# Three split fp32r passes for the second expert product, and an earlier start of the gathered rows

## The chip, the cores and the metric

The kernel runs on one core of one Trainium2 chip. The metric is the device time of one execution in microseconds. The kernel before was timed in three runs: 2528.99, 2518.30 and 2519.91 us, median 2519.91.

## The reference

256 tokens with 2048 features pass through two layers. The first layer and the first part of the second are projections, a gated convolution, causal attention over 8 heads, a 31-tap convolution and a state-space recurrence. The change does not touch them, save for one loop named below. It concerns the last part, a product-key mixture of single-neuron experts:

```python
def peer(h, w_q, sub_keys, u_tab, v_tab):     # h (B,S,2048); both tables 16384 x 2048
        q = (xb @ w_q).reshape(PEER_TOKEN_BLOCK, PEER_HEADS, 2, PEER_HALF)
        s = jnp.einsum('thcd,hcnd->thcn', q, sub_keys).astype(jnp.float32)
        s_top, i_top = lax.top_k(s, PEER_TOPK)
        ...
        best, pos = lax.top_k(cand, PEER_TOPK)
        expert = jnp.take_along_axis(cand_idx, pos, axis=-1)
        gates = jax.nn.softmax(best, axis=-1).astype(xb.dtype)
        u_sel = u_tab[expert]
        v_sel = v_tab[expert]
        act = jax.nn.gelu(jnp.einsum('td,thkd->thk', xb, u_sel))
        return jnp.einsum('thk,thkd->td', gates * act, v_sel)
```

Each token takes 16 experts in each of 8 heads. The result is added to the residual and normalised once more (gain `gfin`).

## The kernel before

**Two ways through the experts.** The first 88 tokens (`NS_`) are done sparsely: for every token and chosen expert the row of the u table and later the row of the v table is gathered from HBM. One gather (`gather`, L1416, an indirect DMA on GpSimd's queue) brings 128 rows, a [128, 2048] buffer of 1 MB. For a u row VectorE forms a dot product with the token's row (L1449); for a v row it adds the row, times its weight, to a sum `acc_s` (L1461, L1463). `GROUPS` puts 32, 32, 16 and 8 tokens on 128 partitions, so there are 88 u gathers and 88 v gathers, in batches of four, a v batch one batch behind its u batch. The other 168 tokens (`NT`) are done densely: all 16384 experts in 128 tiles of 128. `u_step` (L1577) multiplies u tile i with the tokens, 16 matmuls into one bank, and ScalarE applies the gelu (L1580). `weigh` (L1391, L1395) multiplies by a gate table, zero where a token did not choose an expert. `v_step` (L1594) multiplies v tile i with these weights, 16 matmuls into 16 sums `acc[d]`, which stay open in six PSUM banks for all 128 tiles.

**Number formats.** Earlier weight tiles are split: ScalarE copies the tile to an fp32r part (`w_hi`, L189), VectorE subtracts it and writes the fp32r rest (`w_lo`, L195), and a product is hi x hi + hi x lo + lo x hi. `mm_perm` (L278 to L280) does that with three matmuls of 256 columns; `mm_wide` (L293, L294) with one of 512 columns, both activation parts side by side, and one of 256. The expert tiles are not split: they are listed in `whole`, and their products are single f32 matmuls of 168 columns, each of which the chip executes as two instructions.

**Order.** Everything is written out in order by a generator scheduler. `step` first issues loads and splits that lie ahead (`w_ahead`; `LDH` and `LDL` say how far), then the step's matmuls, then lets background generators run: `weave.run`, and `run_paced`, which gives the sparse generator `sparse` 0.78 of a 2350 ns row product per step. Each engine takes its instructions in that order. Weight tiles arrive by SyncE's queue (`w_load`, L183) in the order of the list `order`: 58 u tiles (`NU0`), then v and u tiles in turn until the u tiles end, then v tiles alone. Five raw buffers (`NR`) go round; a buffer is loaded again once the matmuls of its tile have run.

**What precedes the expert stage.** 16 query projection tiles (two in `first_tiles`, 14 by `mm_wide`), then per head the key scores and the top-16 search on VectorE (`topk`, `picks`), first for tokens 0 to 127 (`tt` = 0). After the last head `hand_out` sends expert numbers and later gate values to the gather lists, and `sp_start` begins gathering into five buffers. `gbuild` builds the gate table of the dense tokens by matmuls (L1375), 128 of the 168 tokens through HBM (`gd`), from where `gload` brings back 16 expert tiles at a time.

**The end.** The sparse sums of the last two groups are added to `y` by `join_rows` through PSUM banks 0 and 1; it needs these banks, which the u product also uses, so it asserts that the u product has ended (`u_done`). The last two v tiles are multiplied bank by bank, with transposes and sums of squares between (L1666, L1673), then the rows are scaled and stored.

## Time and profile before

| | |
|---|---|
| runs | 2528.99, 2518.30, 2519.91 us; median 2519.91 |
| profiled execution | 2530.83 us, span from first to last instruction 2528.9 us |
| mean granted TensorE clock | 0.991 |
| HBM read, written | 687.10 MB, 25.91 MB |
| DMA | 719.91 MB, mean 285 GB/s |
| u products (L1577) | 4096 instructions, first at 1229.0 us, last at 2220.0 |
| v products (L1594) | 4096 instructions, first at 1545.4 us, last at 2512.6 |

The profile shows one execution. Its engines are PE (matmuls) and PEld (weight loads) of TensorE, DVE (VectorE), ACT (ScalarE), POOL (GpSimd) and SP (SyncE, DMA issue only). A group's line gives busy time and the mean of one instruction, then the idle time just before its instructions with what ended it. Matmuls overlap in the pipeline, so the time that one takes from its neighbours is the distance of starts, not its duration. In a timeline consecutive instructions of one line are merged (x32), and the first start and the total are shown.

### The profile page before, as it was taken

To read this page: it belongs to the slowest core of one execution; us is meant where nothing else is said; L and a number is where in the kernel's file an instruction comes from. 1 tells how busy PE (TensorE), PEld (TensorE's weight loads), DVE (VectorE), ACT (ScalarE), POOL (GpSimd) and SP (SyncE) were. 2 spreads that over 40 slices of the span, in tenths; PEclk is the share of its full clock that TensorE was granted. 3 is DMA by queue.
4 is the path that set the end of the run, shared out by engine and by line. 5 is a ranking of instruction groups with operands and counts; after the bars stand their busy time and mean duration, and the time that the engine had idled before them with its cause. 6 is when DMAs were issued, how large, how long until landed. Compare 5 with 4: busy or idle time off the path is not lost.

```text
span 2528.9 us, 40512 instructions
## 1 busy us (share of the span) xinstructions
PE 2445.0 (97%) x16864; PEld 2322.2 (92%) x16864; DVE 1586.5 (63%) x2764; ACT 700.2 (28%) x1047; POOL 657.0 (26%) x856
## 2 busy tenths in 40 slices
PE   8999999999999999999998999999999999999997
PEld 7888878899999999988998999999999999999887
DVE  6857777589999987657768874534453434324423
ACT  5544455443334445454201640000000000000002
POOL 1788888310000000140122121212122312022000
PEclk9999999999999999999999999999999999999998
DMA  6455555565555444555599999999999999999983
GB/s 237 168 199 184 183 183 210 193 238 210 199 206 179 183 168 181 185 202 193 215 336 418 370 380 417 421 382 421 418 421 415 396 386 414 365 344 398 387 259 125
DMA packets 108187, 719.91 MB, mean 285 GB/s; under 512 B 13308, under 2 KB 14572, under 8 KB 24668
## 3 DMA queue, kind: packets, MB, share of 16 engines
q1 hardware_dynamic: 65764, 474.57, 49.9%
q0 software_dynamic: 34288, 220.73, 22.3%
q10 hardware_dynamic: 7952, 22.02, 2.4%
q8 instruction: 133, 2.18, 0.3%
q14 instruction: 50, 0.41, 0.0%
HBM read 687.10 MB, written 25.91 MB: 282 GB/s over the span
## 4 chain that ended last, share of the span: by engine, by line
PE 71%; DMA 19%; DVE 7%; issue 2%; ACT 1%; POOL 1%; SPq 0%; DVEq 0%; POOLq 0%; ACTq 0%
PE b L1577 14%; PE b L293 13%; PE b L1594 12%; DMA s<-in_vexp_dram 7%; PE b L294 7%; DMA s<-in_wst_dram 6%; PE b L278 4%; PE b L280 4%; PE b L279 4%; DVE s L195 2%; PE b L271 2%; PE b L423 2%; PE b L270 2%; PE b L269 2%; DMA s<-s 2%
## 5 line engine op out<-in xcount | busy, mean ns | idle before, releaser
L1577 PE MATMUL b<-s,s 128*128 128x168 f32 x4096 | 609.2, 308 | 14.0 <-DMA s<-in_wst_dram 13.6
L1594 PE MATMUL b<-s,s 128*128 128x168 f32 x4096 | 605.1, 307 | 17.3 <-DMA s<-in_vexp_dram 15.9
L1594 PEld LDWEIGHTS b<-s,s 128*128 128x128 f32 x4096 | 588.3, 190 | 30.4 <-issue 27.0
L1577 PEld LDWEIGHTS b<-s,s 128*128 128x128 f32 x4096 | 590.6, 191 | 21.4 <-issue 20.4
L293 PE MATMUL b<-s,s 128*128 128x512 f32 x1680 | 599.7, 400 | 0.0
L294 PE MATMUL b<-s,s 128*128 128x256 f32 x1680 | 472.0, 281 | 9.6 <-DVE s L195 9.6
L195 DVE TENSOR_TENSOR s<-s,s 128x2048 fp32r<-128x2048 f32 x192 | 453.3, 2363 | 27.2 <-issue 12.5
L293 PEld LDWEIGHTS b<-s,s 128*128 128x128 f32 x1680 | 316.1, 188 | 72.8
L189 ACT ACTIVATE s<-s 128x2048 fp32r<-128x2048 f32 x192 | 365.7, 1905 | 9.6 <-DMA s<-in_wst_dram 9.1
L1449 DVE CUSTOM_DVE_ANT_0 s<-s,s 128x2048 f32<-128x2048 f32 x88 | 201.1, 2290 | 261.0 <-DMA s<-in_uexp_dram,rbuf 209.9
L294 PEld LDWEIGHTS b<-s,s 128*128 128x128 f32 x1680 | 317.7, 189 | 13.8 <-DVE s L195 13.0
L1463 DVE SCALAR_TENSOR_TENSOR s<-s,sqsum,s 128x2048 f32<-128x2048 f32 x84 | 197.4, 2350 | 120.8 <-DMA s<-in_vexp_dram,rbuf 120.3
L1580 ACT ACTIVATE s<-b 128x168 f32<-128x168 f32 x128 | 39.1, 307 | 803.7 <-PE b L1577 803.7
L278 PE MATMUL b<-s,s 128*128 128x256 f32 x896 | 256.6, 286 | 0.0
L280 PE MATMUL b<-s,s 128*128 128x256 f32 x896 | 253.5, 283 | 0.0
L279 PE MATMUL b<-s,s 128*128 128x256 f32 x896 | 253.5, 283 | 0.0
L1416 POOL DMA_INDIRECT s<-in_uexp_dram,rbuf x88 | 110.5, 1256 | 394.6 <-DVE s L1463 218.0
L1416 POOL DMA_INDIRECT s<-in_vexp_dram,rbuf x88 | 103.1, 1171 | 316.5 <-DVE sqsum L1449 224.6
L278 PEld LDWEIGHTS b<-s,s 128*128 128x128 f32 x896 | 171.8, 192 | 3.7 <-issue 2.9
L279 PEld LDWEIGHTS b<-s,s 128*128 128x128 f32 x896 | 171.9, 192 | 0.3
L280 PEld LDWEIGHTS b<-s,s 128*128 128x128 f32 x896 | 171.9, 192 | 0.0
L837 POOL TENSOR_TENSOR sqsum<-sqsum,s 128x256 f32<-128x256 f32 x28 | 59.4, 2120 | 389.7 <-ACT s L835 389.7
(310 smaller groups left out, 2511.8 us busy)
## 6 DMA issues: line engine op xcount, KB each, us to landing
s<-in_wst_dram SPq DMA_DIRECT2D x320, 1024.0 KB, 5.0
s<-in_vexp_dram SPq DMA_DIRECT2D x128, 1024.0 KB, 17.4
tabd<-s POOLq DMA_DIRECT2D x32, 256.0 KB, 4.5
s<-tabd ACTq DMA_DIRECT2D x32, 256.0 KB, 3.5
gd<-s ACTq DMA_DIRECT2D x8, 1024.0 KB, 9.9
s<-gd POOLq DMA_DIRECT2D x7, 1024.0 KB, 27.0
xd<-s POOLq DMA_DIRECT2D x4, 1024.0 KB, 9.8
s<-in_bblk_dram ACTq DMA_DIRECT2D x8, 512.0 KB, 3.6
```

The lines of the kernel that those rows point to most:

```text
L189: nc.scalar.activation(hi_of(i), raw_of(i), AF.Copy)
L195: nc.vector.tensor_tensor(out=lo_of(i), in0=raw_of(i), in1=FV(hi_of(i)), op=ALU.subtract)
L278: nc.tensor.matmul(ps, a, xh, start=(j == 0), stop=False)
L279: nc.tensor.matmul(ps, a, xl, start=False, stop=False)
L280: nc.tensor.matmul(ps, b, xh, start=False, stop=(j == len(perm) - 1))
L293: nc.tensor.matmul(ps, a, x2, start=(j == 0), stop=False)
L294: nc.tensor.matmul(ps[:, :T], b, x2[:, :T], start=False, stop=(j == len(perm) - 1))
L1416: nc.gpsimd.indirect_dma_start(out=gb[m % len(gb)][:], out_offset=None, in_=uexp if kind == "u" else vexp, in_offset=bass.IndirectOffsetOn ...
L1449: V.tensor_tensor_reduce(out=buf, in0=buf, in1=x_rep, scale=1.0, scalar=0.0, op0=ALU.mult, op1=ALU.add, accum_out=dots_[:, k:k + 1])
L1463: V.scalar_tensor_tensor(out=acc_s, in0=buf, scalar=a, in1=acc_s, op0=ALU.mult, op1=ALU.add)
L1577: nc.tensor.matmul(ps, raw[:, k * P:(k + 1) * P], nv(k)[:, NS_:T], start=(k == 0), stop=(k == KT - 1))
L1594: nc.tensor.matmul(acc[d], raw[:, d * P:(d + 1) * P], act_at(i), start=False, stop=(i == P - 1 and (d % 3 == 2 or d == KT - 1)))
```

## The change

- v tiles are split like earlier weights: `w_hi` and `w_lo` write to two hi buffers (`HI2`) and two lo buffers (`LO2`), as far as `may_split` allows (two v tiles in all). `prepare` splits the weighted activations of a tile into `ah` and `al`. `v_products` issues three fp32r matmuls of 168 columns for a product. u tiles stay f32.
- Raw buffers come from a free list (`w_free`, `w_slot`); a u tile gives its buffer back after its matmuls, a v tile after its split. One raw buffer and two gather buffers are given up for the split parts when the second product opens (`retired`, `w_retired`), so that four raw and four gather buffers remain. The 2048-column slot 24 becomes two of 1024, of which slot 25 holds `ah` and `al`.
- The order of tiles after the first 58: the other 70 u tiles are spread over the first 112 v tiles (`NV1`) instead of one for one. The pace falls to 0.68 of a row product per step when the second product opens.
- The search hands over expert numbers of the first four heads first (`number`, `told`), after head 4 instead of head 5 has been searched; gathers begin with these for the first group (`gathers`). `sp_start` moves to the end of the query projection. The token rows for the dot products come from HBM (`hrow`), v rows wait for the gate values, and the order of a u batch and a v batch is swapped at a change of group.
- `join_rows` no longer asserts the end of the u product but yields until it has come; `y` is loaded once v tile 84 is past.
- The 14 query projection tiles use `mm_perm` with 256 columns instead of `mm_wide`.
- The gate table lies in HBM in 16 blocks of 8 expert tiles; blocks of 512 KB come back, two of them in one buffer.

```diff
-    WU, NR = 192, 5
+    WU = 192
...
-    hi_of = lambda i: HI[i % len(HI)]
-    lo_of = lambda i: LO[i % len(LO)]
+    HI2, LO2, v_of, n_v = [], [], {}, [0]
+    hi_of = lambda i: HI2[v_of[i] % 2] if i in v_of else HI[i % len(HI)]
+    lo_of = lambda i: LO2[v_of[i] % 2] if i in v_of else LO[i % len(LO)]
+    may_split = lambda i: i not in v_of or (LO2 and v_of[i] - 2 < n_v[0])
...
-        return RAW[i % 3] if i < WU else EARLY[i - WU] if i < WU + 3 else RAW[(i - WU - 3) % NR]
+        return RAW[i % 3] if i < WU else EARLY[i - WU] if i < WU + 3 else S[w_slot[i]]
...
-        if i < WU + 3 + NR:
-            return ws["n"] >= WU
-        return i - NR < ws["n"]
+        return bool(w_free)
...
+        if i >= WU + 3:
+            w_slot[i] = i - WU - 3 if i < WU + 6 else w_free.pop(0)
...
+        if i in v_of:
+            w_release(i)
...
-        while ws["lo"] <= min(i + LDL, last) and ws["dma"] > ws["lo"]:
+        while ws["lo"] <= min(i + LDL, last) and ws["dma"] > ws["lo"] and may_split(ws["lo"]):
...
+        if i in whole:
+            w_release(i)
...
+    hrow = drp.tile([NS_, D], F32, name="hrow")
...
-    gd = drp.tile([NSP, P, P, 16], F32, name="gd")
+    gd = drp.tile([16, P, NSP, 8, 16], F32, name="gd")
...
+        nc.gpsimd.dma_start(hrow, S[18][0:NS_, :])
+        rows(0)
...
+        hs = slice(h, h + 4)
+        nc.vector.scalar_tensor_tensor(out=ab[:, 0, hs], in0=idx[:, 0, hs], scalar=float(P), in1=idx[:, 1, hs],
+                                       op0=ALU.mult, op1=ALU.add)
+        nc.vector.tensor_copy(by_part(ids, hs), parts4(ab[:, 0, hs]))
...
-                if h == 5:
+                if h == 4:
                     yield from picks(tt, 0)
+                    if tt == 0:
+                        number(0)
+                        hand_to(0, 0, 0, 16)
+                        told.add("first")
             yield from picks(tt, 4)
             if tt == 0:
-                hand_out(0)
+                number(4)
+                hand_to(0, 0, 16, 32)
+                for g in range(1, len(GROUPS)):
+                    hand_to(0, g)
+                told.add("all")
...
             if tt == 0:
-                hand_out(1)
+                V.tensor_copy(by_part(abr[:, P:2 * P], slice(0, 8)), parts4(gat))
+                for g in range(len(GROUPS)):
+                    hand_to(1, g)
+                told.add("gates")
...
-                gbufs.append(S[11])
                 gload(0, nc.scalar)
+                gload(1, nc.scalar)
...
-            nc.scalar.dma_start(gd[n], by_expert(n))
...
-    gblk = lambda b: gbufs[b % 2].rearrange("p (n i t) -> p n i t", n=NSP, i=16)
+            nc.scalar.dma_start(gd[:, :, n].rearrange("b p i t -> p b i t"),
+                                by_expert(n).rearrange("p (b i) t -> p b i t", b=16))
+
+    gblk = lambda b: S[11][:, b % 2 * 1024:(b % 2 + 1) * 1024].rearrange("p (n i t) -> p n i t", n=NSP, i=8)
 
     def gload(b, eng):
-        eng.dma_start(gblk(b), gd[:, :, 16 * b:16 * b + 16, :].rearrange("n p i t -> p n i t"))
...
     def weigh(i):
 
...
             nc.vector.tensor_tensor(out=r, in0=r, in1=by_expert(NSP + n)[:, i, :], op=ALU.mult)
             t0 += w
-        if i % 16 == 15 and i // 16 + 2 < 8:
-            gload(i // 16 + 2, nc.gpsimd)
...
+        pair = [("u", j), ("v", j - 1)]
+        if 0 < j < len(batches) and batches[j][0] != batches[j - 1][0]:
+            pair.reverse()
+        for kind, m in pair:
...
+    def gathers():
+
+        while free_b and n_gathered[0] < len(items):
+            kind, g, k = items[n_gathered[0]]
+            if "all" not in told and not ("first" in told and g == 0 and k < 16):
+                return
+            b = free_b.pop(0)
+            nc.gpsimd.indirect_dma_start(
+                out=S[b][:], out_offset=None, in_=uexp if kind == "u" else vexp,
+                in_offset=bass.IndirectOffsetOnAxis(ap=gaddr[:, LCOL[g] + k:LCOL[g] + k + 1], axis=0))
+            flying.append(b)
+            n_gathered[0] += 1
...
+        slots([6, 5, 7, 18, 3, 4])
+        free_b.extend([6, 5, 7, 18])
+        w_free.extend([3, 4])
+        gathers()
...
-            buf = gb[m % len(gb)]
+            while n_gathered[0] <= m or (kind == "v" and "gates" not in told):
+                gathers()
+                yield None
+            b = flying.pop(0)
+            buf = S[b]
...
-            if m + len(gb) < len(items):
-                gather(m + len(gb))
+            if b not in retired:
+                free_b.append(b)
+            if more and s_ready[0] == NH:
+                slots(more)
+                free_b.extend(more)
+                more = []
+            gathers()
...
-                y_rows.append(slots([18])[0][0:NS_, :])
+                while n_v[0] <= 7 * TPS:
+                    yield None
+                y_rows.append(slots([15])[0][0:NS_, :])
...
-        assert u_done[0]
+        while not u_done[0]:
+            yield None
...
-    NU0 = 58
-    for i in range(NU0):
-        order.append((wst[WU + i], plain))
+    NU0, NV1 = 58, 112
+    steps = [("u", i) for i in range(NU0)]
     for i in range(P):
-        order.append((vexp[i * P:(i + 1) * P, :], plain))
-        if NU0 + i < P:
-            order.append((wst[WU + NU0 + i], plain))
-    whole.update(range(WU, WU + 2 * P))
+        steps.append(("v", i))
+        for u in range(NU0 + i * (P - NU0) // NV1, NU0 + (i + 1) * (P - NU0) // NV1):
+            if u < P:
+                steps.append(("u", u))
...
+        order.append((wst[WU + i] if kind == "u" else vexp[i * P:(i + 1) * P, :], plain))
+        if kind == "u":
+            whole.add(WU + n)
+        else:
+            v_of[WU + n] = i
...
-        ps = mmbank2(1)
-        step(lambda wh, wl: mm_wide(ps, wh, wl, pv2, allk), ev_pq(ps, j), TOP)
+        ps = mmbank()
+        step(lambda wh, wl: mm_perm(ps, wh, wl, pv, allk), ev_pq(ps, j), TOP)
+    sp_start()
...
+    def act_split(i):
+
+        o = i % 2 * 2 * NT
+        return S[25][:, o:o + NT], S[25][:, o + NT:o + 2 * NT]
+
+    def prepare(i):
+        ah, al = act_split(i)
+        nc.scalar.activation(ah, act_at(i), AF.Copy)
+        nc.vector.tensor_tensor(out=al, in0=act_at(i), in1=FV(ah), op=ALU.subtract)
+
+    def v_products(i, wh, wl, ds):
+        ah, al = act_split(i)
         for d in ds:
-            nc.tensor.matmul(acc[d], raw[:, d * P:(d + 1) * P], act_at(i), start=False,
+            w = slice(d * P, (d + 1) * P)
+            nc.tensor.matmul(acc[d], wh[:, w], ah, start=False, stop=False)
+            nc.tensor.matmul(acc[d], wh[:, w], al, start=False, stop=False)
+            nc.tensor.matmul(acc[d], wl[:, w], ah, start=False,
                              stop=(i == P - 1 and (d % 3 == 2 or d == KT - 1)))
...
+        if i == NU0 - 10:
+            retired.update([13, 18])
+            w_retired.add(4)
+            if 4 in w_free:
+                w_free.remove(4)
+                w_out_of_use.add(4)
+            free_b[:] = [b for b in free_b if b not in retired]
...
+    while retired & set(flying):
+        next(sp_gen)
...
+    HI2.extend(slots([13, 18], F32R))
+    slots([25], F32R)
+    LO2.extend(slots([4, 22], F32R))
+    weave.pace = 0.68 * 2350
...
-    n_weighed = 0
-    for i in range(P - LAST):
+    n_weighed, n_ready = 0, 0
+    for kind, i in steps[NU0:-LAST]:
+        if kind == "u":
+            u_step(i, 0.0)
+            if i == P - 1:
+                flush()
+                u_done[0] = True
...
+        while n_ready <= min(i + 1, P - 1):
+            prepare(n_ready)
+            n_ready += 1
...
     weave.finish(sp_gen)
...
-    w_ahead(n0 + LAST - 1)
+    w_ahead(n0)
+    while n_ready < P:
+        prepare(n_ready)
+        n_ready += 1
+    parts_w = [(hi_of(n0 + n), lo_of(n0 + n)) for n in range(LAST)]
```

## Rows read from the trace of the kernel before

**Rows 1.** The page's busy time, share and instructions of each engine, whole span.

```profile
PE 2445.0 (97%) x16864; PEld 2322.2 (92%) x16864; DVE 1586.5 (63%) x2764; ACT 700.2 (28%) x1047; POOL 657.0 (26%) x856
```

**Rows 2.** Stage table: us; PE, PEld, DVE, ACT, POOL busy; PEclk, DMA share, GB/s.

```profile
1229.00:1340.00 111.00, 110.85 (x781) 110.59 (x779) 78.57 (x290) 13.00 (x36) 26.48 (x40) 1.00 0.76 279
...
1545.00:2220.00 675.00, 654.44 (x4484) 641.11 (x4483) 287.72 (x474) 22.72 (x83) 153.45 (x136) 1.00 1.00 403
```

**Rows 3.** Groups by line, both expert products: busy us, mean ns, idle and releaser.

```profile
L1577 PE MATMUL b<-s,s 128*128 128x168 f32 x4096 | 609.2, 308 | 14.0 <-DMA s<-in_wst_dram 13.6 <-ACT s L1580 0.4
L1594 PE MATMUL b<-s,s 128*128 128x168 f32 x4096 | 605.1, 307 | 17.3 <-DMA s<-in_vexp_dram 15.9 <-DVE s L1395 0.4 <-DVE s L1463 0.2
```

**Rows 4.** Timeline of PE: start us, us, instructions of one tile each.

```profile
2101.55 4.72 PE L1594 MATMUL b<-s,s 128*128 128x168 f32 x32
2106.11 4.72 PE L1577 MATMUL b<-s,s 128*128 128x168 f32 x32
```

**Rows 5.** Timeline of weight loads, three-pass loop.

```profile
700.18 0.19 PEld L278 LDWEIGHTS b<-s,s 128*128 128x128 f32 x1
700.30 0.19 PEld L279 LDWEIGHTS b<-s,s 128*128 128x128 f32 x1
```

**Rows 6.** Timeline of PE, three-pass loop.

```profile
700.29 0.28 PE L278 MATMUL b<-s,s 128*128 128x256 f32 x1
700.41 0.28 PE L279 MATMUL b<-s,s 128*128 128x256 f32 x1
```

**Rows 7.** Timeline of weight loads, wide loop, first two after an idle PE.

```profile
353.20 0.19 PEld L294 LDWEIGHTS b<-s,s 128*128 128x128 f32 x1 [2.74 <-DVE s L195]
353.31 0.19 PEld L293 LDWEIGHTS b<-s,s 128*128 128x128 f32 x1
```

**Rows 8.** Timeline of weight loads, four in front of 64-column matmuls.

```profile
1123.87 0.52 PEld L365 LDWEIGHTS b<-onesm,s 128*128 128x128 f32 x4 [0.77 <-ACT s L835]
```

**Rows 9.** Timeline of PE, wide loop: 512 and 256 columns in turn.

```profile
353.43 0.39 PE L293 MATMUL b<-s,s 128*128 128x512 f32 x1
353.66 0.28 PE L294 MATMUL b<-s,s 128*128 128x256 f32 x1
353.77 0.40 PE L293 MATMUL b<-s,s 128*128 128x512 f32 x1
```

**Rows 10.** Groups by line: splits, gathered rows, gate weighting.

```profile
L294 PE MATMUL b<-s,s 128*128 128x256 f32 x1680 | 472.0, 281 | 9.6 <-DVE s L195 9.6
...
L195 DVE TENSOR_TENSOR s<-s,s 128x2048 fp32r<-128x2048 f32 x192 | 453.3, 2363 | 27.2 <-issue 12.5 <-ACT s L189 7.8 <-PE b L423 2.6
...
L189 ACT ACTIVATE s<-s 128x2048 fp32r<-128x2048 f32 x192 | 365.7, 1905 | 9.6 <-DMA s<-in_wst_dram 9.1 <-DVE s L305 0.5
...
L1449 DVE CUSTOM_DVE_ANT_0 s<-s,s 128x2048 f32<-128x2048 f32 x88 | 201.1, 2290 | 261.0 <-DMA s<-in_uexp_dram,rbuf 209.9 <-DMA s<-s 51.0
...
L1463 DVE SCALAR_TENSOR_TENSOR s<-s,sqsum,s 128x2048 f32<-128x2048 f32 x84 | 197.4, 2350 | 120.8 <-DMA s<-in_vexp_dram,rbuf 120.3
...
L1391 DVE TENSOR_TENSOR s<-s,s 128x128 f32<-128x128 f32 x128 | 36.4, 284 | 0.1
...
L1395 DVE TENSOR_TENSOR s<-s,s 128x16 f32<-128x16 f32 x256 | 32.4, 168 | 0.0
```

**Rows 11.** DMA issues, whole span: KB each, median us to landing.

```profile
s<-in_vexp_dram SPq DMA_DIRECT2D x128, 1024.0 KB, 17.4
```

**Rows 12.** Single lines: duration ns min/median/max, first and last start us.

```profile
L1375 PE MATMUL b<-s x336: 272/275/275, 1383.6 to 1492.8; 128*128 128x128 f32 x168
...
L1416 POOL DMA_INDIRECT s<-in_uexp_dram,rbuf x88: 939/946/4154, 1259.3 to 2324.3; - x88
...
L1463 DVE SCALAR_TENSOR_TENSOR s<-s,sqsum,s x84: 2333/2352/2354, 1349.9 to 2402.0; 128x2048 f32<-128x2048 f32 x84
...
L1504 POOL DMA_DIRECT2D out_dram<-s x1: 557/557/557, 2478.5 to 2478.5; - x1
...
L1666 DVE TENSOR_TENSOR s<-b,s x6: 315/665/682, 2501.0 to 2516.7; 128x504 f32<-128x504 f32 x5, 128x168 f32<-128x168 f32 x1
```

More of the change, by code (lines that the diff above doesn't have):

```diff
@@ L135, in slots @@
         for k in ks:
-            S[k] = big.tile([P, 2048], dt, tag=f"s{k}", name=f"s{k}")
+            S[k] = big.tile([P, 1024 if k in (24, 25) else 2048], dt, tag=f"s{k}", name=f"s{k}")
         return [S[k] for k in ks]
@@ L173, in raw_free, with w_release @@
             return i - 6 < ws["lo"]
-        if i < WU + 3 + NR:
-            return ws["n"] >= WU
-        return i - NR < ws["n"]
+        return bool(w_free)
+    def w_release(i):
+        k = w_slot.pop(i, None)
+        if k in w_retired:
+            w_out_of_use.add(k)
+        elif k is not None:
+            w_free.append(k)
     def w_load():
         i = ws["dma"]
-        if i == WU + 6:
-            RAW.extend(slots([3, 4]))
+        if i >= WU + 3:
+            w_slot[i] = i - WU - 3 if i < WU + 6 else w_free.pop(0)
         src, dst_view = order[i]
@@ L210, in w_ahead @@
             w_loads()
-        while ws["hi"] <= min(i + LDH, last) and ws["dma"] > ws["hi"]:
+        while ws["hi"] <= min(i + LDH, last) and ws["dma"] > ws["hi"] and may_split(ws["hi"]):
             w_hi()
@@ L228, in body @@
     NRING = 4
-    free_units = [S[24][:, k * T:(k + 1) * T] for k in range(NRING, 8)]
+    free_units = [S[25][:, k * T:(k + 1) * T] for k in range(4)]
     free_pairs = []
@@ L1228, in body, with number, hand_to @@
     LCOL = [0, 64, 128, 160]
-    def hand_out(c):
-        V = nc.vector
-        if c == 0:
-            V.scalar_tensor_tensor(out=flat(ab[:, 0]), in0=flat(idx[:, 0]), scalar=float(P), in1=flat(idx[:, 1]),
-                                   op0=ALU.mult, op1=ALU.add)
-            V.tensor_copy(flat(abu[:, 0]), flat(ab[:, 0]))
-        else:
-            V.tensor_copy(abr[:, P:2 * P], flat(gat))
-        for g in range(2):
-            hand_to(c, g)
-            if c == 0 and g == 0:
-                sp_start()
-        for g in range(2, len(GROUPS)):
-            hand_to(c, g)
-    def hand_to(c, g):
+    ids = mask.bitcast(U32)
+    by_part = lambda ap, hs: ap.rearrange("p (q h j) -> p h q j", q=4, h=8)[:, hs]
+    parts4 = lambda ap: ap.rearrange("p h (q j) -> p h q j", q=4)
+    def number(h):
+        hs = slice(h, h + 4)
+        nc.vector.scalar_tensor_tensor(out=ab[:, 0, hs], in0=idx[:, 0, hs], scalar=float(P), in1=idx[:, 1, hs],
+                                       op0=ALU.mult, op1=ALU.add)
+        nc.vector.tensor_copy(by_part(ids, hs), parts4(ab[:, 0, hs]))
+    def hand_to(c, g, k0=0, k1=None):
         t0, n = GROUPS[g]
@@ L1422, in rows @@
         for q in range(P // n):
-            nc.gpsimd.dma_start(x_rep[n * q:n * q + n, :], S[18][t0:t0 + n, :])
+            nc.gpsimd.dma_start(x_rep[n * q:n * q + n, :], hrow[t0:t0 + n, :])
     def sp_start():
-        assert ws["n"] >= WU and len(q_ready) == KT and s_ready[0] == NH
-        gb.extend(slots([5, 6, 7, 12, 13]))
-        for m in range(len(gb)):
-            gather(m)
-            if m == 0:
-                rows(0)
+        assert ws["n"] == WU
+        slots([6, 5, 7, 18, 3, 4])
+        free_b.extend([6, 5, 7, 18])
+        w_free.extend([3, 4])
+        gathers()
         weave.paced.append(sp_gen)
@@ L1435, in sparse @@
         V = nc.vector
+        more = [12, 13]
         for _ in range(AHEAD):
+            gathers()
             yield None
@@ L1485, in sparse @@
         y = y_rows[0]
+        gb = [S[b] for b in (5, 6, 7, 12)]
         quarters = [gb[q][0:64, :] for q in range(4)]
```

74 lines of the change are left out of this document (35 added, 39 removed).

## The prediction

> **What bounds the kernel now.** I began with the busy shares: TensorE has work on it for 97% of the span, no other engine for more than 63% [rows 1]. I then cut the last half by stage [rows 2]. From 1545 us, where both expert products run, TensorE is busy 654 of 675 us and the 16 DMA engines are busy for the whole stage at 403 GB/s, while VectorE is busy 288 of 675 us. So two resources are near their limit at once. Which one ends last is read from TensorE's idle time in the grouped lines: its two expert groups (L1577 first product, L1594 second) waited 14.0 and 17.3 us, nearly all of it for DMA [rows 3]. That is 31 us in 8192 instructions, so TensorE sets the end and DMA is just behind it.
>
> What TensorE pays has to come from start times, because busy times of pipelined matmuls overlap (307 ns each in the group). One second-product tile starts at 2101.55, the next tile at 2106.11 [rows 4]: 4.56 us for 32 instructions, 142.5 ns each. A product written once (16 per tile) is two f32 instructions, 285 ns; all 128 tiles cost 128 x 4.56 = 583.7 us.
>
> **The change part by part.**
>
> *Three fp32r passes for the second product.* The new tile has 16 x 3 = 48 instructions of 168 columns, each with its own weights. That a repeated operand does not spare its load is seen in the weight loads of the existing three-pass loop: L278 and L279 use the same slice, and each has its own load, 0.12 us after the one before [rows 5]. No row of before shows an fp32r matmul of 168 columns, so I bound it.
> - From above among fp32r rows: the same loop at 256 columns starts an instruction every 0.12 us [rows 6].
> - From below, weights seen: after an idle PE two fp32r weight loads start 353.20 and 353.31, 0.11 apart [rows 7]. A 64-column f32 matmul (L365) still loads four sets of weights in 0.52 us, (0.52 - 0.19) / 3 = 0.11 apart [rows 8], though it streams less than half of the columns that make L1594 take 142.5 ns (64 / 168 x 142.5 = 54). So with few columns the load sets the spacing; I write 111 to 112 ns.
> - From below, weights hidden: 512 columns take 0.23 us and 256 take 0.115 in the wide loop [rows 9], 0.45 ns per column, so 168 columns would be about 75 to 80 ns.
> - Far above: at the f32 price of a whole product, 285 ns per pass.
>
> I take 115 ns, between the 0.111 of the loads and the 0.12 of the only fp32r three-pass row, and nearer to the load because 168 columns stream in less than a load. Tile: 48 x 115 = 5.52 us instead of 4.56. Sum: 128 x 0.96 = **+123 us** on the engine that sets the end (+101 at 111.5 ns, +154 at 120). Three cheap passes lose to two dear ones since each pass buys its own weight load.
>
> An fp32r load takes as long as an f32 one, 0.11 us [rows 7, 8], so the type brings no quicker load. A rule of the Trainium skill could be read the other way: "TensorE: Matmul & The Clock Gate", section "Weight-path perf modes — Fast Weight Load (FWL) and DoubleRow", says that the fast load is on for 128 weights of any type but FP32. If fp32r counted as another type, the spacing would be the 75 to 80 ns above and this term -92 to -123 us; by the measured loads it does not.
>
> *Splitting the tiles.* Each v tile now takes what an fp32r weight tile takes today: 1.91 us on ScalarE (L189) and 2.36 on VectorE (L195). The activations of 168 columns take a short ACT copy (0.3 is my estimate, a sixth of L189's) and a DVE subtraction, a little above the 0.28 of 128 columns (L1391), say 0.33. The gate weighting stays 0.28 + 3 x 0.17 = 0.79 [rows 10]. VectorE per v tile: 2.36 + 0.33 + 0.79 = 3.48 us. To this come gathered rows at 2.35 us each, 0.68 per step instead of 0.78 (the pace). With 0.62 first-product tiles per second-product tile, 1.62 steps hold 5.52 + 0.62 x 4.56 = 8.35 us of TensorE and 3.48 + 1.62 x 0.68 x 2.35 = 6.07 us of VectorE: 73%, hidden. Where two v tiles follow each other the cover is thin: buffers of v tile j+1 come free when TensorE leaves j-1, then ScalarE 0.3 + 1.91, VectorE 2.36 (0.33 beside ScalarE) give 4.6 of 5.52 us; one gathered row in front (2.35) makes it late by about 1.4. Now a DVE instruction that waits for a gather holds the next split behind it, and TensorE waits for that; before, only the weighting stood there, two tiles ahead. The same split in the projections costs TensorE 9.6 us in 105 tiles [rows 10], 0.09 per tile, so 12 us here; 0.5 per tile, 64 us, is my upper end and zero the lower. I take +12. The first v tile can't be split ahead, since its buffers are handed over only when the second product opens: one split in the open, 1.91 + 2.36 and a bit, **+5**.
>
> *DMA.* Bytes stay the same. A v tile's raw buffer is now freed by its split and not by its matmul; with two raw buffers given up, four remain. Per pair of tiles DMA moves 2 x 1.05 + 1.36 x 1.05 = 3.53 MB in 10.1 us, 350 GB/s, against the 403 of today [rows 2]. So most of the 31 us that TensorE waits for tiles goes: **-25** (0 to -31). A tile lands 17.4 us after its issue [rows 11], under full engines; four buffers and 8.35 / 1.62 = 5.15 us per step cover 20.6, enough once the engines are not full.
>
> *Gathers half a list earlier.* The first gather is issued at 1259.3 [rows 12]; I put the first one of the change 30 us earlier (one head and half of the picks less), when the first product starts. That uses DMA when it is at 0.76 [rows 2], with four buffers at first, so at most 4 to 8 MB (10 to 20 us of a full stage) come forward. With TensorE as the bound this buys nothing beyond the -25. Extra rows on VectorE among the top-16 work (78.6 of 111 us busy [rows 2]) may delay the gate table; its last matmul starts at 1492.8 [rows 12], about 50 us before the second product begins at 1545, which cover it: nothing.
>
> *Small moves.* The query projection goes from pairs (353.43 to 353.77 [rows 9], 0.34 to 0.35 us) to three passes of 0.12: 14 tiles x 16 x 0.01 to 0.02 = +3 us. The gate table in 512 KB blocks moves the same bytes on the GpSimd queue; its writes are short runs, hidden: nothing, up to +5 if not.
>
> *The end.* Today the sparse rows' last product starts at 2402.0 and their output leaves at 2478.5, before TensorE's last sums at 2501.0 [rows 12]; 22 us to spare. In the change the first product ends at v tile 112 instead of 70, and the joining of the sparse rows now waits for that. Of 176 row products some 46 can be done when the second product opens (8 before the gate values are there, then 0.78 per step for about 48 steps). The join that waits stands before the last 13, so it is reached after another 117 / 0.68 = 172 steps, ten before the first product's last at step 182. Then 14 steps remain; four go to the join, ten give seven rows. Some six rows (6 x 2.35 = 14 us), a join and four quarter sums (4 x 2.3 = 9 us, priced as a gathered row) stand on VectorE ahead of the last sums, and the joins stand on TensorE before the last two tiles. I take **+15** (0 to +45), since a wait on a gather or a slower start of the rows moves it either way.
>
> Sum: +123 + 3 + 12 + 5 - 25 + 15 = +133 us. The profiled execution took 2530.8 us (span 2528.9), 10.9 above the median of the runs, 2519.9; I add to the median: about **2653 us**.
>
> **The rivals.**
> 1. *Weights do not bind*: a load is quicker, or shared by equal operands, and a narrow pass costs its columns. For it: the times of 512 and 256 columns scale with columns [rows 9]. Against: [rows 5, 7, 8]. A pass is 77 ns, a tile 3.70 us, TensorE -110 us. It decides below 95 ns per pass (285 / 3). DMA then binds: a pair would ask 3.53 MB in 8.26 us, 427 GB/s, more than today's 403. What is left is today's 31 us of waits turned around and the earlier gathers: about -40. Time 2480, faster.
> 2. *VectorE becomes the bound.* For it: in-order waits for gathers of 210 and 120 us today [rows 10]. Against: those waits come from full DMA engines. The price is the upper ends of split and tail, +64 and +45: 2520 + 123 + 3 + 5 + 64 + 45 = 2760.
> 3. *Narrow fp32r passes cost what f32 costs.* No row excludes it, since every fp32r row has 256 columns or more. 48 x 285 = 13.7 us a tile, +1167: about 3690.
> 4. *Cheap passes, all waits gone*: +101 + 3 - 31 = +73 with nothing at the end: 2593. This lies in my own range.
>
> **How the numbers follow.** The forecast with 4 as its lower part 0.72, own range 2590 to 2715; rival 2 0.11; rival 1 0.10; rival 3 0.03; and 0.04 that costs and recovered waits cancel. 0.5% of the median, 12.6 us, is about what a measurement here tells from no change. Faster 0.10, same 0.04, slower 0.86. The range 2580 to 2765 leaves out rivals 1 and 3 and the cancelling case, 0.17.
>
> **What would show it.** The second product's line, three instructions per product, should start every 111 to 120 ns, its tile 5.3 to 5.8 us; below 95 ns the forecast falls. DMA share in that stage should be clearly below 1.0 and near 350 GB/s. TensorE's idle time there should name DVE (the split) and no longer DMA. The last row sums should end behind the last v tile's start. If the line spaces as said and the time is still not slower, a wait that I count as 25 us was larger.

## The result and the profile after

The changed kernel takes 2651.99 us (median of 4 runs, 2651.17 to 2653.83) against 2521.22 us of the kernel before beside it: ratio 1.0515, interval 1.049 to 1.0539, 131 us slower. The forecast was 2653 us. Its sum came out by errors that cancel: the passes cost less than forecast and all waits for tiles went, while the end, the first second-product tile and the gate table cost more. Lines have moved: the first product is L1639, the three passes L1668 to L1670, the splits L198 (ScalarE) and L204 (VectorE), the activations' split L1661 and L1662, the weighted v rows L1509.

The page's busy share of TensorE has hardly moved [rows 1], though the kernel is 5% longer; VectorE rose from 63 to 72%:

```profile
PE 2549.6 (96%) x19136; PEld 2451.5 (93%) x19136; DVE 1899.1 (72%) x3008; ACT 977.7 (37%) x1305; POOL 688.8 (26%) x868
```

The stage table (columns as in [rows 2]) shows where TensorE's limit went. From 1640 to 2300 us it has work for all 660 us and the DMA engines are no longer full, a share of 0.93 and 364 GB/s where 350 was forecast. On both sides of this stretch the granted clock (the column after POOL) falls: 0.89 when the second product opens, where before has 1.00 (shown below the table), and 0.94 from 2300 us on. The 0.74 of the last 29 us is no news, since before has 0.77 in its own last 29.

```profile
1229.00:1340.00 111.00, 111.00 (x786) 111.00 (x785) 95.42 (x318) 13.21 (x36) 34.11 (x45) 1.00 0.88 345
...
1545.00:1640.00 95.00, 92.14 (x666) 91.55 (x664) 49.94 (x70) 23.89 (x30) 12.75 (x10) 0.89 0.76 295
1640.00:2300.00 660.00, 660.00 (x5471) 660.00 (x5470) 440.19 (x626) 190.68 (x223) 136.22 (x119) 1.00 0.93 364
2300.00:2620.00 320.00, 279.21 (x2279) 272.30 (x2279) 210.48 (x294) 93.09 (x102) 61.13 (x60) 0.94 0.81 295
2620.00:2649.00 29.00, 14.83 (x106) 13.27 (x105) 12.18 (x33) 9.11 (x28) 0.00 (x0) 0.74 0.13 48
```

The kernel before, same stretch of the opening:

```profile
1545.00:1640.00 95.00, 95.00 (x668) 94.92 (x667) 45.24 (x72) 3.29 (x12) 24.00 (x26) 1.00 1.01 418
```

The groups of the expert products: the passes wait for no DMA any more [rows 3]; L204 (the split) now waits for the copy ahead of it, and the copy for L1669, the last pass that reads the hi part, so the splits run at the speed at which TensorE frees their buffers.

```profile
L204 DVE TENSOR_TENSOR s<-s,s 128x2048 fp32r<-128x2048 f32 x320 | 745.7, 2332 | 206.1 <-ACT s L198 162.7 <-issue 19.3 <-PE b L293 12.9
L1639 PE MATMUL b<-s,s 128*128 128x168 f32 x4096 | 610.2, 308 | 0.0
L198 ACT ACTIVATE s<-s 128x2048 fp32r<-128x2048 f32 x320 | 609.4, 1906 | 190.9 <-PE b L1669 108.0 <-DMA s<-in_vexp_dram 70.4 <-DMA s<-in_wst_dram 9.4
L1668 PE MATMUL b<-s,s 128*128 128x168 f32 x2048 | 575.8, 281 | 19.7 <-ACT s L1661 18.7 <-ACT s L198 1.0
L1670 PE MATMUL b<-s,s 128*128 128x168 f32 x2048 | 566.8, 277 | 5.2 <-DVE s L204 5.2
```

What TensorE waits for, whole span (us in total, times, longest): two long waits of the end, four for the gate table, and only 5.2 us for the lo parts of v tiles.

```profile
PE b L1668 <- ACT s L1661: 18.7, 1, 18.7
PE b L1571 <- DVE s L1509: 16.8, 1, 16.8
PE b L1404 <- ACT s L1385: 14.6, 4, 4.8
...
PE b L1670 <- DVE s L204: 5.2, 5, 1.9
```

TensorE's timeline shows the pass and then the end: three products (nine instructions) from 2571.02 to 2572.03, 112 ns per start; then the sparse rows' join (L1571) after 16.8 us of idle, a few products, 18.7 us of idle again, and starts 0.21 apart instead of 0.11.

```profile
2571.02 0.27 PE L1668 MATMUL b<-s,s 128*128 128x168 f32 x1
...
2572.03 0.27 PE L1668 MATMUL b<-s,s 128*128 128x168 f32 x1
...
2589.36 5.61 PE L1571 MATMUL b<-s,rconv 128*88 128x512 f32 x8 [16.84 <-DVE s L1509]
...
2614.69 0.51 PE L1668 MATMUL b<-s,s 128*128 128x168 f32 x1 [18.74 <-ACT s L1661]
...
2617.55 0.41 PE L1668 MATMUL b<-s,s 128*128 128x168 f32 x1
2617.76 0.41 PE L1669 MATMUL b<-s,s 128*128 128x168 f32 x1
```

VectorE's timeline of the same place names the work in front of the last splits: the last gathered row, the four quarter sums (L1547, 9.24 us), the row norm, and only then a split.

```profile
2586.96 2.35 DVE L1509 SCALAR_TENSOR_TENSOR s<-s,sqsum,s 128x2048 f32<-128x2048 f32 x1 [0.28 <-DMA s<-in_vexp_dram,rbuf]
...
2595.73 9.24 DVE L1547 TENSOR_TENSOR s<-s,s 64x2048 f32<-64x2048 f32 x4
2607.04 2.29 DVE L1553 TENSOR_TENSOR s<-s,s 88x2048 f32<-88x2048 f32 x1 [2.07 <-ACT s L1552]
...
2614.44 2.29 DVE L204 TENSOR_TENSOR s<-s,s 128x2048 fp32r<-128x2048 f32 x1 [3.87 <-ACT s L198]
```

### The profile page after: what moved, and what is told of

Its sections match the earlier page's. It is cut to its first block, busy times and chain, and to the rows that moved or that the text cites. A ratio compares the mean times of both kernels' runs of the same rounds, so it can differ in the third digit from the quotient of the medians.

```text
span 2649.4 us, 45709 instructions
## 1 busy us (share of the span) xinstructions
PE 2549.6 (96%) x19136; PEld 2451.5 (93%) x19136; DVE 1899.1 (72%) x3008; ACT 977.7 (37%) x1305; POOL 688.8 (26%) x868
## 3 DMA queue, kind: packets, MB, share of 16 engines
q0 software_dynamic: 34640, 221.45, 21.8%
## 4 chain that ended last, share of the span: by engine, by line
PE 84%; DVE 5%; DMA 5%; issue 3%; ACT 2%; POOL 0%; SPq 0%; ACTq 0%; POOLq 0%; DVEq 0%
PE b L1639 20%; PE b L306 11%; PE b L1670 7%; PE b L1668 7%; PE b L1669 7%; PE b L307 6%; PE b L291 5%; PE b L293 5%; PE b L292 5%; DMA gd<-s 2%; DVE s L204 2%; DMA s<-in_vexp_dram 2%; PE b L436 2%; PE b L284 2%; PE b L283 2%
## 5 line engine op out<-in xcount | busy, mean ns | idle before, releaser
L204 DVE TENSOR_TENSOR s<-s,s 128x2048 fp32r<-128x2048 f32 x320 | 745.7, 2332 | 206.1 <-ACT s L198 162.7
L198 ACT ACTIVATE s<-s 128x2048 fp32r<-128x2048 f32 x320 | 609.4, 1906 | 190.9 <-PE b L1669 108.0
L1639 PE MATMUL b<-s,s 128*128 128x168 f32 x4096 | 610.2, 308 | 0.0
L1668 PE MATMUL b<-s,s 128*128 128x168 f32 x2048 | 575.8, 281 | 19.7 <-ACT s L1661 18.7
L1639 PEld LDWEIGHTS b<-s,s 128*128 128x128 f32 x4096 | 591.4, 192 | 0.1
L1670 PE MATMUL b<-s,s 128*128 128x168 f32 x2048 | 566.8, 277 | 5.2 <-DVE s L204 5.2
L1669 PE MATMUL b<-s,s 128*128 128x168 f32 x2048 | 565.7, 276 | 1.8 <-DVE s L1662 1.8
L306 PE MATMUL b<-s,s 128*128 128x512 f32 x1456 | 520.7, 401 | 0.0
L1668 PEld LDWEIGHTS b<-s,s 128*128 128x128 f32 x2048 | 397.9, 194 | 21.1 <-ACT s L1661 18.9
L307 PE MATMUL b<-s,s 128*128 128x256 f32 x1456 | 409.3, 281 | 8.3 <-DVE s L204 8.3
L1670 PEld LDWEIGHTS b<-s,s 128*128 128x128 f32 x2048 | 398.0, 194 | 6.0 <-DVE s L204 6.0
L1669 PEld LDWEIGHTS b<-s,s 128*128 128x128 f32 x2048 | 397.9, 194 | 2.8 <-DVE s L1662 2.1
L306 PEld LDWEIGHTS b<-s,s 128*128 128x128 f32 x1456 | 274.2, 188 | 64.1
L291 PE MATMUL b<-s,s 128*128 128x256 f32 x1120 | 320.7, 286 | 0.0
L293 PE MATMUL b<-s,s 128*128 128x256 f32 x1120 | 317.0, 283 | 0.0
L292 PE MATMUL b<-s,s 128*128 128x256 f32 x1120 | 316.9, 283 | 0.0
L307 PEld LDWEIGHTS b<-s,s 128*128 128x128 f32 x1456 | 275.4, 189 | 12.1 <-DVE s L204 11.4
L1454 POOL DMA_INDIRECT s<-in_uexp_dram,rbuf x88 | 119.9, 1363 | 563.7 <-DVE s L1509 362.3
L1454 POOL DMA_INDIRECT s<-in_vexp_dram,rbuf x88 | 118.3, 1344 | 437.1 <-DVE sqsum L1495 316.0
L291 PEld LDWEIGHTS b<-s,s 128*128 128x128 f32 x1120 | 214.8, 192 | 3.7 <-issue 2.9
L292 PEld LDWEIGHTS b<-s,s 128*128 128x128 f32 x1120 | 214.9, 192 | 0.3
L293 PEld LDWEIGHTS b<-s,s 128*128 128x128 f32 x1120 | 214.8, 192 | 0.0
## 6 DMA issues: line engine op xcount, KB each, us to landing
gd<-s ACTq DMA_DIRECT2D x8, 1024.0 KB, 16.4
s<-gd POOLq DMA_DIRECT2D x14, 512.0 KB, 10.6
```

Source lines behind the costliest of these rows:

```text
L198: nc.scalar.activation(hi_of(i), raw_of(i), AF.Copy)
L204: nc.vector.tensor_tensor(out=lo_of(i), in0=raw_of(i), in1=FV(hi_of(i)), op=ALU.subtract)
L291: nc.tensor.matmul(ps, a, xh, start=(j == 0), stop=False)
L292: nc.tensor.matmul(ps, a, xl, start=False, stop=False)
L293: nc.tensor.matmul(ps, b, xh, start=False, stop=(j == len(perm) - 1))
L306: nc.tensor.matmul(ps, a, x2, start=(j == 0), stop=False)
```

## The experiments

Each is the changed kernel with the edits named; code is cut to the lines that matter. Ratios are to the kernel before, run on the same chip beside it (medians 2524.7 to 2526.3, where it was 2521.2 beside the change). So a difference of medians from the change's 2652 us crosses chips and can be some 5 us off; where it matters the difference by ratios stands beside it.

**1. f32 of the hi part, all splits kept.**

```
-            nc.tensor.matmul(acc[d], wh[:, w], ah, start=False, stop=False)
-            nc.tensor.matmul(acc[d], wh[:, w], al, start=False, stop=False)
-            nc.tensor.matmul(acc[d], wl[:, w], ah, start=False,
+            nc.tensor.matmul(acc[d], FV(wh[:, w]), act_at(i), start=False,
```

> The kernel after, but a second product is one f32 matmul of the hi part with the unsplit activation; all splits are still made, so VectorE, ScalarE, DMA and the order of tiles stay. It leaves out the lo part of the v tiles. Theory (each fp32r pass is held by its own weight load, 112 ns, so three passes cost 336 ns where two f32 instructions cost 285): a v tile is 4.56 us again, the second product loses about 102 us, time 2550, between 2535 and 2575. Rival (the loss is in the splitting on VectorE, the new order and the tail): at least 2630.

Measured: 2536.15 us, ratio 1.0033 (1.0016 to 1.005). With every split and the new order in place, going back to two f32 instructions takes 116 us off (122 by ratios), so VectorE's added work is not the cost. A second-product tile takes 4.56 us again (L1668, 2018.91 to 2023.47 on TensorE's timeline):

```profile
2018.91 4.72 PE L1668 MATMUL b<-s,s 128*128 128x168 f32 x32
2023.47 4.72 PE L1639 MATMUL b<-s,s 128*128 128x168 f32 x32
```

TensorE's waits, though: 25.1 us for the copies, of which one of 18.6 us at the end, where the passes of the change wait 18.7 us. That the end costs something whatever the passes cost is seen here. The waits for tiles have not come back: from 1640 to 2300 us TensorE has work for 659.58 of 660 us while the DMA engines are full, at 400 GB/s.

```profile
PE b L1668 <- ACT s L198: 25.1, 7, 18.6
PE b L1571 <- DVE s L1509: 17.2, 1, 17.2
```

```profile
1640.00:2300.00 660.00, 659.58 (x4627) 659.07 (x4626) 483.02 (x688) 207.13 (x245) 121.39 (x138) 1.00 1.00 400
```

**2. Three passes of 84 columns.** To see whether the load or the columns set the spacing; half of the dense tokens are left out.

```
+            h = NT // 2
-            nc.tensor.matmul(acc[d], wh[:, w], ah, start=False, stop=False)
+            nc.tensor.matmul(acc[d][:, 0:h], wh[:, w], ah[:, 0:h], start=False, stop=False)
...
```

> The kernel after with 84 columns in each of the three passes instead of 168; the sums of the second half of the dense tokens are left out. Theory (weight load): start spacing stays 110 to 112 ns, a v tile 5.3 to 5.4 us, time 2652 within 10. Rival (columns set the pace of a pass, as they do at 256 and 512): spacing falls towards 70 ns, v tile under 4 us, time under 2600.

Measured: 3099.57 us, ratio 1.2265 (1.2217 to 1.2313). Both expectations missed the time, by well over 400 us, since neither had the clock in it. The mean granted clock of the execution is 0.83, where the change has 0.98: some 1050 us at the lower level against 100. An estimate from these shares, with work taking twice as long there, is 475 us, enough for the whole difference. The loads answer the question all the same. On the timeline of weight loads they start 0.11 apart at 1800 us, as with 168 columns, not 0.07; at 2000 us each takes 0.33 instead of 0.19 and they start 0.21 apart:

```profile
1799.87 0.19 PEld L1669 LDWEIGHTS b<-s,s 128*128 128x128 f32 x1
1799.98 0.19 PEld L1670 LDWEIGHTS b<-s,s 128*128 128x128 f32 x1
...
1999.87 0.33 PEld L1669 LDWEIGHTS b<-s,s 128*128 128x128 f32 x1
2000.08 0.33 PEld L1670 LDWEIGHTS b<-s,s 128*128 128x128 f32 x1
```

The stage table has TensorE busy for all of 1040 us, without a single wait in its list, and a granted clock of 0.68, a mean of the 2.4 and 1.2 GHz levels, with the lower one in some two thirds of the time:

```profile
1560.00:2600.00 1040.00, 1040.00 (x5964) 1040.00 (x5965) 482.46 (x685) 204.73 (x241) 150.88 (x129) 0.68 0.67 252
```

**3. The gate table in long write runs again** (8 KB instead of 512 bytes; the reads take the short ones).

```
-    gd = drp.tile([16, P, NSP, 8, 16], F32, name="gd")
+    gd = drp.tile([NSP, P, P, 16], F32, name="gd")
```

> The kernel after with the gate table laid out in HBM as before (written in 8 KB runs per partition, read back in 512-byte runs, 8 tiles at a time). Theory (writes in 512-byte runs take longer, ScalarE waits for them 12.8 us before it can refill a staging buffer, and TensorE's gate matmuls wait 14.6 us for ScalarE): 10 to 15 us less, 2637 to 2642. Rival (these waits come from the extra row work and the order on ScalarE): no change, 2650 to 2654.

Measured: 2641.43 us, ratio 1.0453 (1.043 to 1.0476), 10.6 us less than the change, as expected (16 by ratios). Its TensorE waits have no L1404 any more, and its second product opens 312.1 us after the first one where the change takes 327.5, 15.4 us sooner. From issue to landing (KB each, median us) a table's write takes 16.4 us in the change and 10.5 here, 9.9 before:

```profile
gd<-s ACTq DMA_DIRECT2D x8, 1024.0 KB, 16.4
```

```profile
gd<-s ACTq DMA_DIRECT2D x8, 1024.0 KB, 10.5
```

The Trainium skill, "DMA: Bandwidth & Descriptors", section "Specifications", gives 512 bytes as the least transfer for line rate. These two rows do not agree: at 512 bytes the same megabyte landed 6 us later than in 8 KB runs. The DMA engines were mostly busy with other traffic around these writes; what short writes cost by themselves was not measured.

**4. The first product ends earlier** (at v tile 96 instead of 112, pace 0.78 instead of 0.68).

```
-    NU0, NV1 = 58, 112
+    NU0, NV1 = 58, 96
-    weave.pace = 0.68 * 2350
```

> The kernel after with the first product ended at v tile 96 instead of 112 and the pace kept at 0.78 of a row product per step. Theory (the sparse rows finish behind the last v step and TensorE waits 17 and 19 us for them): both waits go, 25 to 40 us less, 2612 to 2627. Rival (VectorE is so full that more rows per step delay the splits of v tiles): TensorE's waits for the lo split grow from 5 us to over 30, time 2640 or more.

Measured: 2615.64 us, ratio 1.035 (1.0321 to 1.0379): 36 us of the change's time is its end (42 by ratios; 30 by the waits behind 2300 us in the two traces). The wait for the sparse rows (L1571) is gone from TensorE's list and the other is 10.1 us; with more rows per step in between, the waits for splits did not grow (3.6 us against 5.2):

```profile
PE b L1668 <- ACT s L1661: 10.1, 1, 10.1
...
PE b L1670 <- DVE s L204: 3.6, 3, 1.9
```

**5. The split undone**: f32 from the raw tile, no hi and lo buffers, raw buffers free at the matmul, pace 0.78; order, early gathers and gate table as in the change. Since no buffers are given up for split parts, six gather buffers stay (before: five, in the change four from the second product on).

```
-            nc.tensor.matmul(acc[d], wh[:, w], ah, start=False, stop=False)
...
+            nc.tensor.matmul(acc[d], raw[:, w], act_at(i), start=False,
-        while n_ready <= min(i + 1, P - 1):
-            prepare(n_ready)
```

> Only the three passes and the splits of the second product's tiles are undone (f32 from the raw tile, raw buffers free at the matmul, pace 0.78); the two-to-one order, the earlier gathers and the gate table's new place stay. Theory (the passes are the cost, the rest of the change is near zero): an instruction starts every 142.5 ns again, and the 25 us that TensorE waited for the splits with f32 of the hi part (2536) go: 2512 us (2495 to 2530), with 10 to 15 us of the gate table's waits and some wait for the sparse rows' join still in it. Rival A (the DMA waits that the passes had covered come back in full, 31 us): 2530 to 2550. Rival B (the order and the end cost as much as the passes): over 2560.

Measured: 2548.74 us, ratio 1.0098 (1.0081 to 1.0116). The first expectation missed; the time is that of rival A, but by two causes. The DMA waits came back, 21.8 us where before has 29.5, and the end still holds TensorE, 12.9 us in one wait, now at the last sums (L1740). So the 18.6 us of the first experiment look like work of the end and not of the splits; they moved.

```profile
PE b L1740 <- DVE s L1733: 17.1, 5, 12.9
PE b L1664 <- DMA s<-in_vexp_dram: 15.4, 40, 2.8
PE b L1404 <- ACT s L1385: 9.3, 3, 4.0
...
PE b L1636 <- DMA s<-in_wst_dram: 6.4, 22, 1.0
```

**6. Order and gate table undone too.** What stays of the change is the earlier gathers, six gather buffers instead of five, the order of u and v batches, one early row write, the query projection and gate blocks of 8 tiles.

```
-    NU0, NV1 = 58, 112
+    NU0, NV1 = 58, 70
-    gd = drp.tile([16, P, NSP, 8, 16], F32, name="gd")
+    gd = drp.tile([NSP, P, P, 16], F32, name="gd")
```

> As the run before it with the gate table written in long runs as before the change and the tiles one to one again (first product ends at v tile 70): what stays is the gathers from half of the heads on, hrow's early write and the query projection's three passes. Theory: the gate table's wait (10.6 us) and the join's wait (17 us) go, so 2490 us (2478 to 2510), faster than before by 0.5 to 1.5%, since the gathered bytes that are moved ahead of 1340 us are missing from the stage in which DMA is full. Rival (bytes that are moved forward buy nothing, as the forecast had it for the change): 2515 to 2530, no change.

Measured: 2511.92 us, ratio 0.9951 (0.9938 to 0.9965), 12 us faster than before and the best of all; 2 us over the first expectation's window and 3 under the rival's. TensorE's DMA waits are 20.3 us instead of the 29.5 of before [rows 3], and VectorE's idle time for u rows is half of [rows 10], 103 against 210 us; whether the earlier start or the sixth buffer does it was not separated. Groups by line:

```profile
L1494 DVE CUSTOM_DVE_ANT_0 s<-s,s 128x2048 f32<-128x2048 f32 x88 | 200.8, 2289 | 103.3 <-DMA s<-in_uexp_dram,rbuf 103.3
```

**7. The change with both mended parts** (edits 3 and 4 together).

> The changed kernel with both mended parts: long runs of the gate table, and the first product ending at v tile 96 with pace 0.78. If the two costs lie in different places and add up: 2652 - 10.6 - 36.4 = 2605 us (2598 to 2612). If the second only takes up slack that the first gives back: 2612 to 2620. In either case slower than before by over 3%, since the passes' 102 us stay.

Measured: 2600.67 us, ratio 1.0312 (1.0292 to 1.0331). The two costs add up and lie in different places: against the change its trace is 21 us shorter between the first starts of the two products and 30 us in waits behind 2300 us. Its profiled execution lies 66 us above the one before. Counted by starts as in the table further on, the passes cost 103, the first second-product tile and the clock behind it 13 and the end 3; waits and clock from 1640 to 2300 us give 34 back, the earlier opening of the second product 13 and the switches between the products 8. So the passes cost more than what is left, and the waits that went pay for part of them.

**8. Three passes of 128 columns.** The last 40 dense tokens are left out.

```
+            h = 128
-            nc.tensor.matmul(acc[d], wh[:, w], ah, start=False, stop=False)
+            nc.tensor.matmul(acc[d][:, 0:h], wh[:, w], ah[:, 0:h], start=False, stop=False)
...
```

> Three passes of 128 columns instead of 168 (the last 40 dense tokens are left out of the second product). With 84 columns the granted clock fell to the lower level for about half of the stage though TensorE always had work; with 168 it did not. Theory A (passes are bound by the weight load, and the clock holds at 128 columns): spacing 111 to 112 ns, 2645 to 2655 us, the granted clock of 1640 to 2300 at 1.00. Theory B (the fewer the columns behind one load, the more of the stage runs at the lower level): granted clock 0.80 to 0.95 there, 2700 to 2900 us. Theory C (columns do bind at 168 columns): spacing below 108 ns, under 2635 us.

Measured: 2671.5 us, ratio 1.0585 (1.0524 to 1.0646), over theory A's window and under B's. That is the middle of two runs only, 2655.42 and 2687.59 us (mean granted clock 0.975 and 0.962): the first lies 0.4 us over A's window, and the trace is of the second. Its spacing of 109 to 114 ns (median 112) and its granted clock of 1.00 from 1640 to 2300 us are A's. The clock goes to the 1.2 GHz level at 2517 us, about 1 us behind a wait of 0.55 us for a split, and stays there for the next 64 us although TensorE waits for nothing in them:

```profile
2515.95 0.33 PE L1671 MATMUL b<-s,s 128*128 128x128 f32 x1 [0.55 <-DVE s L204]
2516.11 0.27 PE L1669 MATMUL b<-s,s 128*128 128x128 f32 x1
...
2517.08 0.42 PE L1671 MATMUL b<-s,s 128*128 128x128 f32 x1
2517.30 0.41 PE L1669 MATMUL b<-s,s 128*128 128x128 f32 x1
```

```profile
2517.00:2581.00 64.00, 64.00 (x302) 64.00 (x302) 31.47 (x53) 14.78 (x15) 4.84 (x5) 0.50 0.54 196
```

Columns do not bind at 128 (C falls): 40 fewer columns per pass gained nothing.

**9. Two f32 instructions of 84 columns, splits kept.** Half of the dense tokens are left out again.

```
+            h = NT // 2
+            nc.tensor.matmul(acc[d][:, 0:h], FV(wh[:, w]), act_at(i)[:, 0:h], start=False,
```

> The second product as two f32 instructions of 84 columns instead of 168, all splits kept (the second half of the dense tokens is left out); it stands against 2536 us with 168 columns in f32 and 3100 us with 84 columns in three fp32r passes. Theory (a weight load ahead of every instruction costs 111 to 112 ns whatever the type): 111 to 113 ns between starts at the higher clock level where 168 columns took 142.5. If the clock holds, DMA binds (its share was 1.00 with 168 columns) and the time is 2480 to 2540 us. Rival A (few columns behind each load let the clock fall whatever the type): granted clock under 0.85 in 1640 to 2300 and 2600 to 2800 us. Rival B (a f32 load is longer than a fp32r one, or its cost is hidden): spacing over 120 or under 90 ns.

Measured: 2512.87 us, ratio 0.9955 (0.9934 to 0.9976). Of 4096 starts 3422 are 111 or 112 ns after the one before: an f32 instruction with half of the columns costs what an fp32r pass costs, so the load sets both. A tile on TensorE's timeline goes from 2003.46 to 2007.09, 3.63 us:

```profile
2003.46 3.80 PE L1669 MATMUL b<-s,s 128*128 128x84 f32 x32 [0.54 <-ACT s L198]
2007.09 4.76 PE L1639 MATMUL b<-s,s 128*128 128x168 f32 x32
```

The granted clock is 0.93 from 1640 to 2300 us, with TensorE waiting in places (34.5 us); rival A's fall under 0.85 did not come there.

## Why the prediction was right, step by step

In the two profiled executions the span grew by 120.5 us (2528.9 to 2649.4). Start times of TensorE's instructions split this by stretch. A start that comes 1.4 to 2.2 times the undisturbed spacing (142.5 ns in f32, 111.7 in a pass) behind the one before is put down to the lower clock, a longer one to a wait; what goes beyond the spacing is counted.

| Term | Forecast | Trace |
|---|---|---|
| pass spacing, 6144 starts | +123 | +102.5 (686.3 against 583.8) |
| query projection | +3 | +1.6 (first u 1229.03, then 1230.58; 1226.3 to 1230.4 in other runs of the same code, so not clear of noise) |
| gate table, up to the first pass | 0 (to +5) | +11.1: waits 14.6 new, 8.1 gone; the rest mostly lower clock there and 1 in front of the first pass |
| first v tile, to 1640 us | +5 | +12.3: waits 2.2, clock 10.1 |
| 1640 to 2300 us: DMA and split waits | -25 + 12 | -34.2: waits -31.5, clock -2.7 |
| after 2300 us | +15 | +33: waits +32, clock +1 |
| switches between the two products, 70 each way | not in it | -8.1 |
| small differences of spacing | not in it | +2 |
| sum | +133 | +120.5 |

The medians differ by 131 us and not by 120: the profiled execution of before was 10.9 us above its own median. What made it so was not looked for; that the forecast, put on the median, came within 1 us is thereby partly luck, and so is the sum: its terms are off by 7 to 21 us, in both directions.

- *Passes.* Mechanism right, and shown: the spacing is the same at 84, 128 and 168 columns and in either type (experiments 2, 8, 9), and the weight loads have it too. The size was off. I took 115 ns between 111 and 120; it is 111.7, the bound read from [rows 7, 8]. The three-pass row of 0.12 [rows 6] has 256 columns, which is a stream and not a load. Here fp32r loads start 0.11 us apart, as f32 loads do, so the type got no quicker one. The Trainium skill, "TensorE: Matmul & The Clock Gate", section "Weight-path perf modes — Fast Weight Load (FWL) and DoubleRow", has the fast load on for 128 weights of any type but FP32. The trace agrees with it only if fp32r counts as FP32 there. A fixed price of about 111 ns for every instruction, whatever its load, would look the same as a load that binds; a row of before speaks against it. There 16 f32 instructions of 256 columns, each with its own load of only 32 columns of weights and laid side by side (`tile_position`), take 1.07 us; with 0.38 for the last, that is (1.07 - 0.38) / 15 = 0.046 from start to start:

```profile
566.76 1.07 PE L903 MATMUL b<-s,s 128*32 128x256 f32 x16
```

- *Switches.* Not in the forecast. A first-product tile in front of a pass takes 4.47 us (2000.05 to 2004.52) where before has 4.56 [rows 4]; 70 switches each way give 8 us back.

```profile
2000.05 4.76 PE L1639 MATMUL b<-s,s 128*128 128x168 f32 x32
2004.52 0.35 PE L1668 MATMUL b<-s,s 128*128 128x168 f32 x1
```

- *Rivals.* Weights do bind, so rival 1 fell; VectorE is not the bound (experiment 1), so rival 2 fell as a whole, though most of its tail did come; a pass is not at the f32 price, so rival 3 fell. Rival 4 had the right price of a pass and all DMA waits gone, and failed by leaving out the end and the opening.
- *DMA.* All of it went, not 25 of 31 us; a tile lands in 7.4 us instead of 17.4 [rows 11]. The reason given, that a slower second product asks for fewer bytes per us, is not shown to be the one that counts. In experiment 1 the second product is as quick as before and the DMA engines are full, and the waits for tiles are gone all the same (0.3 us in its list, and 6.5 for copies up to the end); in experiment 5, also in f32, 21.8 us are back. Between these two lie the split with its buffers, the pace (0.68 and 0.78) and the number of gather buffers (four and six); which of them takes the waits away stays open.
- *Splits.* 5.2 us where I took 12, and none of it from 1640 to 2300 us. The thin cover of 1.4 us per row hardly ever ran out.
- *First v tile.* The split in the open was priced (5) and the clock behind it was not. The loads of the first v tile go from 0.19 to 0.33 us at 1562.5, behind waits of 0.99 (at 1558.05) and 1.87 (at 1560.38), and 10.1 us are lost at the lower clock:

```profile
1562.27 0.19 PEld L1669 LDWEIGHTS b<-s,s 128*128 128x128 f32 x1
...
1562.70 0.33 PEld L1669 LDWEIGHTS b<-s,s 128*128 128x128 f32 x1
1562.91 0.33 PEld L1670 LDWEIGHTS b<-s,s 128*128 128x128 f32 x1
```

- *The end.* The cost that was set too low by most. The forecast counted the rows left and named the two waits, then took a third of its upper bound because a wait might move it either way. The trace has 16.8 and 18.7 us of them, and experiment 4 gives 36 us back for an earlier end. Experiment 1 has the same end in f32 (33 us more of waits than before behind 2300 us), so the passes do not cause it. The work that I had listed (rows 14, quarter sums 9) stands there nearly as counted; not listed were the row norm and the copy behind it, 9.5 us from the end of the quarter sums (2604.97) to the split (2614.44).
- *Gate table.* Put at nothing, since it has 50 us of cover before the second product. The cover was the wrong one: TensorE's own gate matmuls wait for the buffer that the short-run write holds (L1404 for L1385, ScalarE for the write 12.8 us). Long runs give 10.6 us of the time back (experiment 3; 16 by ratios), and 15.4 in the trace up to the second product.
- *Earlier gathers.* Put at nothing because TensorE would be the bound. In the change nothing tells them apart. With f32 they and the other small parts together are worth about 12 us (experiment 6), with 9 us fewer DMA waits; a sixth gather buffer is among these parts, so the gain is not shown to be the earlier start's.

By ratios, the steps are: gathers and small moves -12 us (experiment 6), order with gate table +37 (from there to experiment 5), split with its passes, pace and gather buffers +105 (from there to the change). In the frame of the three passes, mending order and gate table gives 51 us back (experiment 7); so these parts do not quite add up across frames, and I cannot say which of the two numbers is the order's own.

## What to carry to other kernels

Price a matmul by its weight load first: where fewer columns stream than a load takes, splitting one product into more passes costs one load for each, in f32 as in fp32r. When a wait goes, look for a run that keeps the supposed cause away before naming it: the DMA waits went with a quick second product too. When a stage has a bound at its end, add up the list of work in front of the last instruction and take that sum, not a share of it. A small reshaping of a write is free only if no engine waits for its buffer.

## What the runs showed of the hardware

- A weight load of 128 by 128 starts 0.11 us after the one before at the 2.4 GHz level, in f32 with 84 columns as in fp32r with 84, 128 and 168; at 1.2 GHz it is 0.21 (experiment 2).
- In fp32r with 84 columns the granted clock fell to 1.2 GHz again and again while TensorE waited for nothing (0.68 in 1040 us). With 128 it was 1.00 from 1640 to 2300 us, fell behind a wait of 0.55 us at 2517 us and stayed down for 64 us of work without a wait (one of two runs was traced). With 168 it was 1.00 from 1640 to 2300 us and fell where the second product opens and at the end, each time behind waits.
- In all six traces with fp32r passes the clock fell within 5 us of the first pass (0.70 to 0.91 from 1530 to 1640 us); in the two with f32 and the splits kept, which have the wait of 0.98 or 0.99 us there but not the one of 1.87, it stayed at 1.00. Experiment 9 had 0.93 from 1640 to 2300 us, with waits in between. What decides it was not settled.
